# One inference step of a hybrid encoder: norm of the last tile, load of the convolution state and first sums of a down group rearranged

## The chip, the cores and the metric

The kernel runs on one core of a Trainium2 chip. The metric is the device time of one execution in microseconds. The engines are named as in the profile: PE (TensorE, matrix products), PEld (its weight loads), DVE (VectorE), ACT (ScalarE), POOL (GpSimd) and SP (SyncE, which issues most transfers). Lines such as L787 are lines of the kernel before.

## What is computed

One trunk layer over 1024 prompt frames and 32 sample frames (1056 columns in all, D_MODEL = 1024), all in float32:

```python
h = rmsnorm(x, g_mix) * (1 + sc1) + sh1
u = h @ w_in                                    # q, k, v, mLSTM parts, gates
ya = band_attention(...)                        # 8 heads of 64
xpad = concat([conv_left, qk_in])               # conv_left: state_conv for the sample, zeros for the prompt
conv = silu(sum(xpad[:, j:j + T] * conv_w[j] for j in range(4)) + conv_b)
...                                             # mLSTM, merge, output projection
x = x + gt1 * (merged @ w_out)
h2 = rmsnorm(x, g_ffn) * (1 + sc2) + sh2
g, up = split(h2 @ w_gate_up)
x = x + gt2 * ((silu(g) * up) @ w_down)         # d_ff = 2816, 22 rows of 128
y = x * rsqrt(mean(x * x) + 1e-6) * g_final     # the final norm
```

## The kernel before

**Tiling.** Activations lie with features on the 128 partitions and the 1056 frames on the free axis, cut in three thirds of 352 columns (`TILES`, `thirds`); `cut` = 704 is the start of the last third. Each float32 product is made of three passes over operands that are split in a high and a low part: `split_to` copies the high part on ACT (L394) and subtracts on DVE or POOL for the low part (L395).

**Order.** The order on PE, ACT, DVE and POOL is the order in which the program writes its instructions. SP's transfers are placed by the framework, as early as it reckons them to be free to start. `Weights` keeps a list of weight blocks: `use` calls `advance`, which loads and splits the blocks ahead, four tiles at most. Side jobs (attention, adaLN) are generators that are moved on by `side.tick()` between matmuls.

**Input projection.** `segs` is a list of segments; each calls a function first, then runs weight blocks while a side job goes on. Segment 3 (k, v, q of the last head pair and four gate blocks) comes before segment 4, which begins with `mlstm_setup` (L775): it fills `tri`, `maskbig` and other small tiles on POOL, loads the convolution state (24 rows of 128) into a scratch tile (L785), transposes it on PE (L787) and copies it to `scol` on DVE (L788). Then `vm_block(0)` starts its matmuls (L825).

**Down projection.** The first two thirds use 6 plain rows (`w_d0`, L1967) and two groups of 8 rows, each as 2x2 blocks with seven products instead of eight (`Seven`, `seven_down`). A product is 12 matmuls (`times`, L1726). Four of the seven products start on one of three fresh accumulators or go onto one in use: T2 and T3 onto B11's, B22 onto T1's, and T4 onto B11's again, after the second block of the next output; each finished product is added to the output rows by DVE (L1989). The operands of a group are sums of the activations (`subtract`, L1860, on DVE; for group 0 every other one on POOL) and are then split. The sums of the weight blocks are made by POOL (L1284).

**The plan.** This preparation is a list `steps` of (due beat, units, action), made by `plan_group`. `beside()` is called after each product of 12 matmuls and each fourth k step of the plain rows: it counts a beat (`through`) and runs the steps at the head of the list that are due, up to 2 units a beat (3 beside the plain rows). A fetch costs no unit, a sum or a split one. The list is strictly in order. Beat 12 (`BEFORE`) is the end of the last gate and up block, beat 36 (`FIRST`) the end of the plain rows. A group needs 8 fetches, 8 first sums, 4 splits (B11), 8 second sums and 24 splits; split results go to freed places, which have a due beat of their own (`free`).

**End.** The last third is done row by row, 8 rows (`w_d1`, L2082): 66 matmuls in three weight blocks (`chunks`), then x2 = acc * gt2 + x2 on DVE (L2090). Beside rows 0 to 6, `finish_some` norms the first two thirds. For the last third, `Finish` (three tiles of 128, 128 and 96 frames) transposes x2 back to frames (L2028), sums squares on ACT (L2029), sums, scales by 1/D, adds EPS and raises to -1/2 on POOL (L2036 to L2038), multiplies by the result and by g_final on DVE (L2044), and stores on SP (L2048). Rows 0 to 6 are taken before the last row's matmuls, row 7 after them.

## Time and profile before

| | us |
|---|---|
| median of three runs | 1645.67 |
| lowest and highest run | 1642.75, 1647.21 |
| the profiled execution | 1642.54 |
| its span, first to last instruction | 1640.6 |
| mean granted clock of PE | 0.995 |

The profile shows one execution. Its first part gives each engine's busy time; the waits say who stood for whom and for how long; the timeline lists instructions in order of time, merged where they repeat, with the idle time before them and what ended it in brackets; windows give the busy time of each engine in a stretch. A wait for several semaphores is put down to the one that came last.

### The profile page before, as it was taken

How to read it: one execution, taken by the hardware profiler on the slowest of the kernel's cores; microseconds unless marked ns; L12 is line 12 of the kernel's file. 1: busy time of each engine (PE TensorE's matmuls, PEld its weight loads, DVE VectorE, ACT ScalarE, POOL GpSimd, SP SyncE). 2: the span in 40 equal slices, each digit the busy share in tenths (PEclk: the TensorE clock that was granted, in tenths of full speed). 3: DMA queues.
4: the chain of work that ended last, by engine and by line, in shares of the span. 5: the costliest groups of instructions: out<-in, count | busy, mean ns of one | idle time of the engine just before them, and what ended most of it. 6: DMA issues, size and time to landing. Idle time of an engine off the chain costs nothing.

```text
span 1640.6 us, 27517 instructions
## 1 busy us (share of the span) xinstructions
PE 1589.7 (97%) x10324; PEld 1566.7 (95%) x10324; DVE 1121.0 (68%) x2100; ACT 780.8 (48%) x1732; POOL 535.7 (33%) x540
## 2 busy tenths in 40 slices
PE   7989999999999999999999998999999999999997
PEld 6989999999999999999999988999999999999997
DVE  6756564546776744546655689889888986698754
ACT  3456454543455544444434645454545444444443
POOL 1234333333332311000012155566565742233101
PEclk9999999999999999999999999999999999999999
DMA  9732323232222332584453211313222236427453
GB/s 344 251 98 75 111 75 106 67 126 75 84 83 78 67 94 66 131 273 152 128 151 109 91 53 39 105 53 104 79 82 88 78 102 216 141 65 238 134 157 123
DMA packets 210326, 192.45 MB, mean 117 GB/s; under 512 B 10570, under 2 KB 180530, under 8 KB 209170
## 3 DMA queue, kind: packets, MB, share of 16 engines
q1 hardware_dynamic: 205970, 188.60, 36.8%
q10 hardware_dynamic: 4224, 2.10, 0.4%
q8 instruction: 81, 1.33, 0.4%
q14 instruction: 51, 0.42, 0.1%
HBM read 152.19 MB, written 41.63 MB: 118 GB/s over the span
## 4 chain that ended last, share of the span: by engine, by line
PE 79%; DVE 8%; ACT 3%; issue 2%; DMA 1%; POOL 1%; DVEq 0%; POOLq 0%; ACTq 0%
PE mm L428 35%; PE psb L1726 24%; PE psb L2082 5%; PE mm L825 3%; PE psb L1967 3%; PE psV L725 2%; PE psS L667 1%; DVE wsp L395 1%; PE psT L694 1%; DVE s L395 1%; DVE s L1576 1%; DVE s L1989 1%; DVE sl L1563 1%; DVE st L681 1%; PE psV L1059 1%
## 5 line engine op out<-in xcount | busy, mean ns | idle before, releaser
L428 PE MATMUL mm<-s,wsp 128*128 128x352 f32 x4104 | 690.4, 324 | 5.8 <-DVE t L1657 1.9
L428 PEld LDWEIGHTS mm<-s,wsp 128*128 128x128 f32 x4104 | 656.8, 188 | 9.0 <-DVE stg L518 2.3
L1726 PE MATMUL psb<-s,wsp 128*128 128x352 f32 x2544 | 422.0, 323 | 11.4 <-DVE s L1989 5.5
L1726 PEld LDWEIGHTS psb<-s,wsp 128*128 128x128 f32 x2544 | 410.9, 189 | 14.4 <-issue 6.1
L395 DVE TENSOR_TENSOR wsp<-wraw,wsp 128x512 fp32r<-128x512 f32 (+1 forms) x284 | 246.0, 884 | 136.0 <-ACT wsp L394 134.2
L394 ACT ACTIVATE wsp<-wraw 128x512 fp32r<-128x512 f32 x340 | 201.5, 617 | 147.6 <-PE psb L1726 84.5
L687 POOL TENSOR_SCALAR st<-st,mx 128x640 f32<-128x640 f32 (+5 forms) x72 | 57.0, 791 | 193.7 <-DVE mx L686 179.5
L1141 DVE SCALAR_TENSOR_TENSOR t<-wa,cmix,t 128x512 f32<-128x512 f32 x112 | 88.8, 797 | 8.9 <-DMA wa<-in_w_ada_dram 8.5
L395 POOL TENSOR_TENSOR wsp<-wraw,wsp 128x512 fp32r<-128x512 f32 x56 | 73.8, 1339 | 52.4 <-ACT wsp L394 52.0
L2082 PE MATMUL psb<-s,wsp 128*128 128x352 f32 x528 | 86.7, 324 | 0.0
L2082 PEld LDWEIGHTS psb<-s,wsp 128*128 128x128 f32 x528 | 84.7, 188 | 0.0
L681 DVE CUSTOM_DVE_ANT_0 st<-psS,bias 128x640 f32<-128x640 f32 (+5 forms) x72 | 44.5, 618 | 57.8 <-PE psS L667 44.9
L1726 PE MATMUL psb<-x,wsp 128*128 128x352 f32 x432 | 80.2, 325 | 2.3 <-DVE x L1576 2.3
L682 ACT ACTIVATE st<-st,mx 128x640 f32<-128x640 f32 (+5 forms) x72 | 47.9, 666 | 67.5 <-DVE mx L681 67.5
L1676 POOL TENSOR_TENSOR t<-t,sl 128x352 f32<-128x352 f32 x18 | 17.4, 969 | 185.3 <-ACT sl L1674 185.3
L1726 PEld LDWEIGHTS psb<-x,wsp 128*128 128x128 f32 x432 | 71.5, 189 | 2.8 <-DVE x L1576 2.8
L701 ACT ACTIVATE pT<-psT 128x640 fp32r<-128x640 f32 (+3 forms) x80 | 38.7, 494 | 72.1 <-PE psT L694 55.1
L1764 DVE TENSOR_TENSOR t<-t,psb 128x352 f32<-128x352 f32 x120 | 60.4, 512 | 5.2 <-PE psb L1726 4.8
L1361 POOL TENSOR_TENSOR wraw<-wraw 128x512 f32<-128x512 f32 x25 | 37.1, 1482 | 76.8 <-DVE wsp L395 75.8
L706 DVE TENSOR_TENSOR pT<-psT,pT 128x640 fp32r<-128x640 f32 (+3 forms) x80 | 44.0, 559 | 20.5 <-ACT pT L701 20.4
L1361 POOL TENSOR_TENSOR wraw<-wraw,raw 128x512 f32<-128x512 f32 x33 | 55.8, 1704 | 0.9
L825 PE MATMUL mm<-s,s 128*128 128x264 f32 (+3 forms) x432 | 54.9, 283 | 0.0
(340 smaller groups left out, 2334.2 us busy)
## 6 DMA issues: line engine op xcount, KB each, us to landing
wraw<-in_w_in_dram SPq DMA_DIRECT2D x40, 512.0 KB
wraw<-in_w_gate_up_dram SPq DMA_DIRECT2D x33, 512.0 KB
wa<-in_w_ada_dram SPq DMA_DIRECT2D x64, 256.0 KB
wraw<-in_w_down_dram SPq DMA_DIRECT2D x32, 512.0 KB
a_d<-t SPq DMA_DIRECT2D x22, 528.0 KB
g_d<-t SPq DMA_DIRECT2D x16, 528.0 KB
x<-xres SPq DMA_DIRECT2D x16, 528.0 KB
t<-g_d SPq DMA_DIRECT2D x16, 528.0 KB
```

Source lines behind the costliest of these rows:

```text
L394: act.activation(dst[:, 0], src, AF.Copy)
L395: eng.tensor_tensor(dst[:, 1], src, f(dst[:, 0]), op=ALU.subtract)
L428: pe.matmul(pt[:, :hi - lo], wt[(w0 + k) // 4][:, a, (w0 + k) % 4], xt[k][:, b, lo:hi], start=(k == 0 and q == 0), stop=(k == n - 1 and q ...
L681: dve.tensor_tensor_reduce(so, sv, bi, -1.0, 3.0e38, ALU.add, ALU.min, mx[:n, 1:2])
L687: pool.tensor_scalar(st[:n, :w], st[:n, :w], mx[:n, 3:4], 1.0, op0=ALU.mult, op1=ALU.mult)
L825: pe.matmul(pt[:n, :wd], hs[k][:, a, i * P:i * P + n], whl[b][:, k, :wd], start=(k == 0 and q == 0), stop=(k == KD - 1 and q == 2))
L1141: dve.scalar_tensor_tensor(ac[:, c], wa, cmix[:, c, k:k + 1], ac[:, c], op0=ALU.mult, op1=ALU.add)
L1361: pool.tensor_tensor(a(dst), a(x), a(y), op=op)
L1726: pe.matmul(acc, wt[:, a, k], x[k][:, b], start=(start and not onto and k == 0 and q == 0), stop=(stop and k == 3 and q == 2), skip_group_ ...
L1764: dve.tensor_tensor(c, c, y, op=ALU.add if sign > 0 else ALU.subtract)
L1967: pe.matmul(acc, wt[k // 4][:, u, k % 4], piece_of[k, i][:, v], start=(k == 0 and q == 0), stop=(k == KP - 1 and q == 2))
L2082: pe.matmul(acc, wt[(k - k0) // 4][:, u, (k - k0) % 4], piece_of[k, 2][:, v], start=(k == 0 and q == 0), stop=(k == NF - 1 and q == 2))
```

## The change

The convolution state is loaded by a new function, `conv_state`, at the start of segment 3, into the first 24 rows of `tri`, and `mlstm_setup` begins with its transpose and copy, before `tri` is filled.

`plan_group` takes a beat for the first sums of its own (`sums_at`). Group 0 keeps its beats. Group 1's fetches are due at beat 27 and its 8 first sums at beat 30, where they were due at beats 36 and 38. Since the list is in order, the steps at the end of group 0 that are due at beat 36 or later (one split, which waits for a freed place) are put behind these sums (`behind`). All other steps of group 1 remain due at beat 38 or later.

For the last third a class `End` takes the place of the three `Finish`. Rows 0 to 6 are transposed and squared after the first weight block of the last row instead of before it (`ahead`). There POOL also adds their two partial sums and EPS (1/D is in the scale of the squares), and DVE multiplies the first 512 columns by g_final. After the last row (`last`), the last block is transposed and squared, POOL adds and takes the power tile by tile, ACT scales the first 512 columns and issues their stores on its own queue, DVE multiplies the other 512 by both factors, and SP stores them.

```diff
@@ -772,7 +772,13 @@
     qk = [None] * MH
     hm_n = [None, None]
 
+    def conv_state():
+        sp.dma_start(tri[:24], state_conv[0, 0].rearrange("j (r c) -> (j r) c", c=P))
+
     def mlstm_setup():
+        pt = mmt()
+        pe.transpose(pt[:, :24], tri[:24], ident[:24, :24])
+        dve.tensor_copy(scol, pt[:, :24])
         pool.memset(tri, 1.0)
         pool.affine_select(out=tri, in_=tri, compare_op=ALU.is_ge, fill=0.0, base=0,
                            pattern=[[1, P]], channel_multiplier=-1)
@@ -781,11 +787,6 @@
                            pattern=[[1, P]], channel_multiplier=-1)
         pool.memset(GT9, 0.0)
         sp.dma_start(bif, bass.AP(b_if.tensor, b_if.offset, [[0, P], [1, 8]]))
-        scr = tmpt((24, P))
-        sp.dma_start(scr, state_conv[0, 0].rearrange("j (r c) -> (j r) c", c=P))
-        pt = mmt()
-        pe.transpose(pt[:, :24], scr, ident[:24, :24])
-        dve.tensor_copy(scol, pt[:, :24])
         pool.memset(vms[:, :, :, P:P + 1], 1.0)
 
     def vm_block(pr):
@@ -1241,7 +1242,7 @@
         (nothing, b_qkv(0), None, 0),
         (nothing, mix(b_qkv(1), b_gates(0, 2)), lambda: attention(0), ATT_STEPS),
         (nothing, mix(b_qkv(2), b_gates(2, 4)), lambda: attention(1), ATT_STEPS),
-        (nothing, b_qkv(3) + b_gates(4, 8), lambda: attention(2), ATT_STEPS),
+        (conv_state, b_qkv(3) + b_gates(4, 8), lambda: attention(2), ATT_STEPS),
         (mlstm_setup, [vm_block(0), conv_block(0), conv_block(4), conv_block(1), conv_block(5)],
          lambda: attention(3), ATT_STEPS),
         (open_mls, [vm_block(1), conv_block(2), conv_block(6), conv_block(3), conv_block(7)],
@@ -1845,7 +1846,7 @@
         steps.append((max(need, after), 1, run))
         return x
 
-    def plan_group(g, fetch_at, work_at):
+    def plan_group(g, fetch_at, sums_at, work_at, behind=()):
 
 
         def block(p, i):
@@ -1855,16 +1856,17 @@
             src = a_d[KP + g * KD + p][:, :cut]
             steps.append((fetch_at, 0, lambda: sp.dma_start(x2[p][:, :cut], src)))
 
-        def subtract(dst, x, y):
+        def subtract(dst, x, y, at=work_at):
             eng = pool if g == 0 and len(steps) % 2 else dve
-            steps.append((work_at, 1, lambda: eng.tensor_tensor(block(*dst), block(*x), block(*y), op=ALU.subtract)))
+            steps.append((at, 1, lambda: eng.tensor_tensor(block(*dst), block(*x), block(*y), op=ALU.subtract)))
 
         for p in range(KD):
             fetch(p)
 
         for p in range(4):
-            subtract((p, 2), (p, 1), (p, 0))
-            subtract((p, 1), (p + 4, 1), (p, 1))
+            subtract((p, 2), (p, 1), (p, 0), sums_at)
+            subtract((p, 1), (p + 4, 1), (p, 1), sums_at)
+        steps.extend(behind)
         freed = [split_step(work_at, block(p, 0), operands[g]["B11"], p) for p in range(4)]
         for p in range(4):
             subtract((p, 0), (p + 4, 1), (p, 2))
@@ -1883,8 +1885,13 @@
         for k in range(KP):
             for i in range(2):
                 free.append((FIRST, split_step(4, x2[k][:, thirds[i]], piece_of, (k, i))))
-        plan_group(0, 9, BEFORE + 2)
-        plan_group(1, FIRST, FIRST + 2)
+        plan_group(0, 9, BEFORE + 2, BEFORE + 2)
+
+
+        behind = []
+        while steps[-1][0] >= FIRST:
+            behind.insert(0, steps.pop())
+        plan_group(1, FIRST - 9, FIRST - 6, FIRST + 2, behind)
         at = FIRST + 28
         raws = {}
 
@@ -2047,6 +2054,50 @@
                     out = y_sample[0, u - S:v - S] if q else y_prompt[0, u:v]
                     sp.dma_start(out[:, cs], y[u - self.a:v - self.a, cs])
 
+    class End:
+
+
+
+        def __init__(self):
+            self.cuts = [(a, min(a + P, T)) for a in range(cut, T, P)]
+            self.py = [(bank(512), bank(512)) for _ in self.cuts]
+            self.st = sl_pool[0].tile([P, 4, 3], F32, tag="est", name=nm("est"), bufs=1)
+            pool.memset(self.st, 1.0)
+            self.ys = [tmpt((P, D)) for _ in self.cuts]
+
+        def take(self, j0, j1, part):
+            for i, (a, b) in enumerate(self.cuts):
+                h, n = j0 // 4, b - a
+                py = self.py[i][h]
+                for j in range(j0, j1):
+                    pe.transpose(py[:n, (j - 4 * h) * P:(j - 4 * h + 1) * P], x2[j][:, a:b], ident)
+                act.activation(self.ys[i][:n, j0 * P:j1 * P], py[:n, (j0 - 4 * h) * P:(j1 - 4 * h) * P], AF.Square,
+                               scale=D ** -0.5, accum_out=self.st[:n, part, i:i + 1])
+
+        def ahead(self):
+            self.take(0, 4, 0)
+            self.take(4, KD - 1, 1)
+            st = self.st
+            pool.tensor_tensor(st[:, 0], st[:, 0], st[:, 1], op=ALU.add)
+            pool.tensor_scalar(st[:, 0], st[:, 0], 1.0, EPS, op0=ALU.mult, op1=ALU.add)
+            for y, py, (a, b) in zip(self.ys, self.py, self.cuts):
+                dve.tensor_tensor(y[:b - a, :512], py[0][:b - a], gB[:b - a, :512], op=ALU.mult)
+
+        def last(self):
+            self.take(KD - 1, KD, 2)
+            st = self.st
+            for i in range(3):
+                pool.tensor_tensor(st[:, 0, i:i + 1], st[:, 0, i:i + 1], st[:, 2, i:i + 1], op=ALU.add)
+                pool.tensor_tensor(st[:, 3, i:i + 1], st[:, 0, i:i + 1], mhalf[:, 0:1], op=ALU.pow)
+            for i, (y, py, (a, b)) in enumerate(zip(self.ys, self.py, self.cuts)):
+                n, r = b - a, st[:b - a, 3, i:i + 1]
+                act.activation(y[:n, :512], y[:n, :512], AF.Copy, scale=r)
+                dve.scalar_tensor_tensor(y[:n, 512:], py[1][:n], r, gB[:n, 512:], op0=ALU.mult, op1=ALU.mult)
+                for eng, cs in ((act, slice(0, 512)), (sp, slice(512, D))):
+                    for q, u, v in col_segments(a, b):
+                        out = y_sample[0, u - S:v - S] if q else y_prompt[0, u:v]
+                        eng.dma_start(out[:, cs], y[u - a:v - a, cs])
+
     def finish_some(ranges):
         for j in range(KD):
             dve.scalar_tensor_tensor(x2[j][:, :cut], cs[j], gt2[:, 0, j:j + 1], x2[j][:, :cut],
@@ -2069,9 +2120,7 @@
     for j in range(KD):
         if j == KD - 1:
             side.drain(job)
-            ends = [Finish(a, min(a + P, T)) for a in range(cut, T, P)]
-            for x in ends:
-                x.take(0, j)
+            end = End()
         acc = bank()
         for w, (k0, k1) in zip(w_d1[j], chunks):
             wt = W.use(w)
@@ -2084,16 +2133,14 @@
                 if k % 2 == 1:
                     side.tick()
             W.used(w)
+            if j == KD - 1 and k0 == 0:
+                end.ahead()
         while steps:
             steps.pop(0)[2]()
         for c, a, b in col_segments(cut, T):
             dve.scalar_tensor_tensor(x2[j][:, a:b], acc[:, a - cut:b - cut], gt2[:, c, j:j + 1], x2[j][:, a:b],
                                      op0=ALU.mult, op1=ALU.add)
-    for x in ends:
-        x.take(KD - 1, KD)
-        x.scale()
-    for x in ends:
-        x.put()
+    end.last()
     close_sl()
     pb_cm.__exit__(None, None, None)
```

## Rows read from the trace of the kernel before

**Rows 1.** The page, part 1: busy us, share of the span, instructions.

```profile
PE 1589.7 (97%) x10324; PEld 1566.7 (95%) x10324; DVE 1121.0 (68%) x2100; ACT 780.8 (48%) x1732; POOL 535.7 (33%) x540
```

**Rows 2.** Waits of PE, whole span: us in total, times, longest.

```profile
PE psb L1726 <- DVE s L1989: 5.5, 4, 2.7
...
PE mm L787 <- DMA t<-in_state_conv_dram: 2.2, 1, 2.2
```

**Rows 3.** Timeline at the conv state: start, us, engine, line, tiles, idle before.

```profile
371.13 0.21 POOL L776 MEMSET tri<- 128x128 f32 x1
...
372.62 0.32 SPq L785 DMA_DIRECT2D t<-in_state_conv_dram  x1
...
374.28 0.24 PE L787 MATMUL mm<-ident,t 24*128 24x24 f32 x1 [2.18 <-DMA t<-in_state_conv_dram]
```

**Rows 4.** Timeline of PE alone, first down group of seven products.

```profile
1429.98 15.73 PE L1726 MATMUL psb<-s,wsp 128*128 128x352 f32 x96 [2.73 <-DVE s L1989]
1446.02 8.28 PE L1726 MATMUL psb<-s,wsp 128*128 128x352 f32 x48 [0.30 <-DVE s L1989]
1455.54 23.51 PE L1726 MATMUL psb<-s,wsp 128*128 128x352 f32 x145 [1.24 <-DVE s L1989]
```

**Rows 5.** Timeline of DVE and POOL in the same stretch.

```profile
1414.81 1.39 DVE L395 TENSOR_TENSOR wsp<-wraw,wsp 128x512 fp32r<-128x512 f32 x2 [3.67 <-ACT wsp L394]
...
1420.01 1.30 POOL L1284 TENSOR_TENSOR t<-wraw,wraw 128x512 f32<-128x512 f32 x1 [4.96 <-issue]
...
1425.20 2.18 DVE L1860 TENSOR_TENSOR x<-x 128x352 f32<-128x352 f32 x2
...
1428.33 1.07 DVE L1860 TENSOR_TENSOR x<-x 128x352 f32<-128x352 f32 x2
1429.32 0.51 DVE L1989 TENSOR_TENSOR s<-s,psb 128x352 f32<-128x352 f32 x1
...
1431.35 0.51 DVE L1989 TENSOR_TENSOR s<-s,psb 128x352 f32<-128x352 f32 x1
...
1434.41 0.96 DVE L395 TENSOR_TENSOR s<-x,s 128x352 fp32r<-128x352 f32 x2
...
1442.29 3.15 DVE L1860 TENSOR_TENSOR x<-x 128x352 f32<-128x352 f32 x2
```

**Rows 6.** Timeline of SP's own queue, the second group's fetches and a load.

```profile
1404.74 1.48 SPq L1856 DMA_DIRECT2D x<-a_d  x3
1411.16 5.48 SPq L1268 DMA_DIRECT2D wraw<-in_w_down_dram  x2
```

**Rows 7.** Windows: length, busy of PE, PEld, DVE, ACT, POOL, clock, DMA share, GB/s.

```profile
1404.00:1416.00 12.00, 12.00 (x76) 12.00 (x75) 3.99 (x6) 3.73 (x8) 5.42 (x4) 1.00 0.71 236
```

**Rows 8.** Timeline of the last row and of the tail.

```profile
1617.19 0.60 ACT L2029 ACTIVATE t<-psb 128x512 f32<-128x512 f32 x1 [2.75 <-PE psb L2028]
1617.31 1.60 PEld L2028 LDWEIGHTS psb<-ident,x 128*128 128x128 f32 x15 [0.23 <-DVE x L2090]
...
1620.31 1.68 ACT L394 ACTIVATE wsp<-wraw 128x512 fp32r<-128x512 f32 x3
...
1631.27 0.20 POOL L2036 TENSOR_TENSOR fst<-fst 128x1 f32<-128x1 f32 x1 [12.65 <-ACT t L2029]
...
1631.83 0.55 POOL L2038 TENSOR_TENSOR fst<-fst,mhalf 128x1 f32<-128x1 f32 x1
...
1632.41 4.09 DVE L2044 SCALAR_TENSOR_TENSOR t<-psb,fst,t 128x512 f32<-128x512 f32 x6 [1.92 <-POOL fst L2038]
...
1633.19 4.97 SPq L2048 DMA_DIRECT2D out_dram<-t  x8
```

**Rows 9.** Windows of the tail, two halves of the stores.

```profile
1634.25:1636.75 2.50, 0.00 (x0) 0.00 (x0) 2.25 (x4) 0.00 (x0) 0.73 (x2) 0.50 1.01 382
1636.75:1639.25 2.50, 0.00 (x0) 0.00 (x0) 0.00 (x0) 0.00 (x0) 0.00 (x0) 0.50 0.66 164
```

**Rows 10.** Instructions of L525, issues on ACT's queue: ns min/median/max.

```profile
L525 ACTq DMA_DIRECT2D out_dram<-stg x8: 378/403/448, 77.6 to 298.5; - x8
```


## Prediction

> **What bounds the kernel now.** I read the busy times first: TensorE (PE) multiplies for 97% of the span [rows 1]. Time is therefore lost only where PE stands, so the second view is the list of PE's waits, and each part of the change is held against its line there [rows 2]. The third is the timeline around each wait, to see what PE stood for and what stood in front of that on the other engine: the conv state [rows 3], the first sums of the second down group [rows 4 to 7]. Last comes the timeline after PE's final matmul, where the chain runs DVE, POOL, DVE, SP, DMA and PE is idle anyway [rows 8 to 10].
>
> **Conv state.** The load of 12 KB is issued at 372.62, when PE has already finished the gate blocks, and PE's transpose starts at 374.28 after 2.18 us of idle time [rows 3]. After the change the load is issued one segment earlier, into `tri`, which nothing else uses yet; that segment is 7 weight blocks long, so it has landed. The transpose itself (0.24 us) stays. Removed: 2.2 us. Is something else late then? The first vm matmuls need `wl` from POOL, which was done before 371.13, since POOL had already begun its memsets then [rows 3]. POOL gets a new wait: memset of `tri` must follow PE's transpose (about 372.3), so POOL's memsets and selects begin 1.2 us later than 371.13, and so, at most, do the low halves of the next conv weights (L395) queued behind them; their matmuls come only after the whole vm block, nine units of work later. DVE's copy of the state, and what stood behind it, moves forward with PE. On SP one issue of 0.32 us goes from here to a place with nothing waiting on it. The scratch buffer that is no longer taken only frees a slot. I take **-2.2 us**; bounds -1.0 (those 1.2 us of POOL met in full) and -2.5 (the copy on DVE, 0.3, gained as well).
>
> **First sums of the second group.** Four waits of PE for DVE's adds make 5.5 us [rows 2]; three of them are 2.73, 0.30 and 1.24 us [rows 4], the fourth, the 1.2 us left of the 5.5, lies in the second group. I count in beats, one product of 12 matmuls: 23.51 us for 145 matmuls is 1.95 us a beat; the 96 matmuls from 1429.98 are beats 41 to 48, the 48 from 1446.02 beats 49 to 52 [rows 4]. With two units of planned work in it, DVE needs 2.03 us for a beat (from one add, 1429.32, to the next, 1431.35) [rows 5], more than PE, so its adds fall behind, and a product that goes onto an old accumulator must wait until the add has read it. Before: beats 38 to 51 carry two units each (8 first sums, 4 splits, 8 second sums, 7 splits: 27 units). After: 8 units are gone from there, 19 are left, in beats 38 to 47.
>
> The *later* waits, 0.30 (after beat 48) and 1.24 (after beat 52), fall when POOL's sums hold DVE up as well (two subtractions take 3.15 us at 1442.29) [rows 4, 5]. At that point the changed plan has nothing left for DVE but weights and adds, 1.1 us of a beat (2.03 less a pair of splits, 0.96 [rows 5]). I book both as gone: -1.5.
>
> The *first* wait, 2.73 us before beat 41, I do not book. Beat 41 adds B22's product onto T1's accumulator. The wait ends when DVE's add of 1429.32 is done (1429.83), and PE resumes at 1429.98 [rows 4, 5]. What stands before that add is beats 38 and 39, two units each. After the change they are still full: the four splits of B11 move up into them. A pair of splits takes 0.96 us where a pair of sums takes 1.07 [rows 5], so 0.2 us is won for two pairs, and the pair that took 2.18 took it because POOL was summing too [rows 5]. So about 2.5 us stays.
>
> *Where the 8 sums go:* beats 30 to 32, behind beat 28 or so of DVE's queue, from 1404.7 on. DVE is busy 3.99 of 12 us between 1404 and 1416 [rows 7], so 8.0 are free. 8 sums at 0.54 (half of 1.07 [rows 5]) are 4.3 us; POOL has four sums there [rows 7], and a pair on DVE that met POOL took 2.18 instead of 1.07 (1425.20 against 1428.33 [rows 5]), 1.1 more; four meetings make 8.7 us in the worst case, that is until 1416.7. Queued behind them on DVE are the low halves of the first group's first two weight blocks (1.39, at 1414.81 in the row [rows 5]), due at PE by 1419.4: done by 1418.1 at the worst. I take 0, and 1 us as the bound, for a last fetch that lands late. The sums wait for eight fetches. Their place in the plan moves from beat 36 to 27, but SP already issued the last of them at 1404.74 to 1406.2, long before beat 36 (1419) [rows 6]: SP's order is not the program's. The last should land by about 1413 (estimate: three of 128 x 704 words and the weight block issued just before them are 1.6 MB, 6.8 us at the 236 GB/s of this stretch [rows 7], from 1406.2). The load of 1411.16 and its successor wait for buffers that DVE's weight halves free, so they come up to 1.9 us later, and POOL's next sums with them (1420.01 [rows 5]), still within the two-unit beats. Sum for the group -1.5 - 0.2 = **-1.7 us**; bounds +1 (above) and -5.5 (all four waits go).
>
> **The last row.** The 21 transposes of the finished rows move from before the row's 66 matmuls to behind its first 24. PE does the same work; what goes is the wait for the previous row's DVE step, 0.23 us [rows 8]. The six squares on ACT took 3.1 us (1617.19 to 1620.31 [rows 8]) and now stand before the split of the row's third weight block. Before that block's turn PE has 24 matmuls, 3.9 us, and the transposes themselves, 1.6 us (the row of 1617.31); squares and the block's first split (0.6 on ACT, 0.7 on DVE) are 4.4. The three DVE multiplications (0.7 each, as in the tail) fit beside them. **-0.2**; bounds -0.3 and +0.6.
>
> **The tail.** Before: POOL's first add at 1631.27, power at 1631.83, then six DVE operations of 0.68 from 1632.41 to 1636.50, and SP's eight issues end at 1638.16 [rows 8]. The 1/D factor and EPS are now applied earlier, so the power follows 0.28 us sooner (DVE at 1632.1), and a tile costs POOL one add and one power, some 0.8 us: tiles are ready at 1632.1, 1632.9 and 1633.7. DVE does three operations instead of six and ends near 1634.5; SP issues four and ends near 1635.6. ACT scales the other halves (0.6 us each, as 128x512 copies [rows 8]) and issues in between, 0.40 us per issue of 128 rows [rows 10], the last two, of fewer rows, some 0.5: 1632.1 + 3 x 0.6 + 2 x 0.4 + 2 x 0.5 and waits of 0.3 give 1636.0. Issues thus end 2.1 us sooner. But the bytes also count. 352 rows of 4 KB are 1.44 MB. While the stores were of 128 rows the 16 DMA engines were full at 382 GB/s; in the second half, of 64 and 32 rows, they moved 164 GB/s at a busy share of 0.66, so full engines would move about 250 [rows 9]. 1.05 MB at 382 and 0.39 MB at 250 are 2.7 + 1.6 = 4.3 us; all at 382 are 3.8. The stores can begin near 1633.9 (0.3 sooner), so they end between 1637.7 and 1638.2, where they ended at 1639.25 [rows 9]: 1.0 to 1.6 sooner. I take **-1.3 us**; bounds -0.3 (a rival, below) and -2.1 (the issues alone).
>
> The Trainium skill's "DMA: Bandwidth & Descriptors" (section "Issuing engines are not separate DMA queues") speaks against this part: starting DMAs from several engines saves only the sequencer's issue time, usually small, since all run on the same 16 DMA engines. By that rule alone the second queue would bring almost nothing.
>
> **Sum.** -2.2 - 1.7 - 0.2 - 1.3 = -5.4 us. The profiled execution took 1642.54 for a span of 1640.6, so it would become 1637.1; it lies 3.1 us under the median of the runs, 1645.67, from which the prediction is made: **1640.3 us**, 0.33% faster. A measurement of this kernel can tell about 0.3%, 4.9 us, from no change.
>
> **Rivals.**
> *The first wait goes too* (13%). For it: two of the three operations ahead of the add were lengthened by POOL, and POOL's sums may come later. Against: the beats stay full. -5.4 - 2.5 gives 1637.8.
> *The second group wins nothing* (15%). POOL's sums, not DVE's, set the late waits: one pair took 3.15 us [rows 5]. -5.4 + 1.7 gives 1642.0.
> *The stores are bound by the DMA engines* (12%). In their second half they moved 164 GB/s, not 382 [rows 9]. If that rate belongs to transfers of 64 and 32 rows whoever issues them, the stores begin and end 0.3 us sooner: -5.4 + 1.0 gives 1641.3. Against: the engines were idle a third of that half, so SP's issues set the pace there. The page's rule named above would give this case.
> *Slower: the sums hold weights up* (10%). Place: DVE's queue between beat 28 and the first seven-product block. If SP puts five of the fetches behind the load it issued at 1411.16 [rows 6], which waits for a DVE half, the last lands not near 1413 but near 1421 (2.3 MB at 236 GB/s are 9.8 us), the sums end at 1422.5, and the first weight half behind them (0.7) makes PE wait 3.8 us from 1419.4; DVE begins the group with that lag, so the first wait can grow by 2.5 and the 1.5 of the late ones stays. Together +7.8, against -5.4: 1648.1. A landing up to 1416 costs nothing; from about 1419 on it outweighs the gains, and every us more adds one.
>
> **How the numbers follow.** Forecast 50% (38 of it past the bound, since 5.4 is only 0.5 us over it), the others as given; of the last, half lands later still and past the bound. Faster by over 0.3%: 38 + 13 = 0.51. Within: 12 + 15 + 12 + 5 = 0.44. Slower: 0.05. The range reaches from the first rival to the second and third and some way to the last, and takes in a median of three from runs that spread over 4.5 us (1.5 us each side): 1635.8 to 1644.4.
>
> **What would show it.** Right: no PE wait for the conv state; PE's wait near the fifth product of the first group still over 2 us, those at beats 48 and 52 gone; the eight subtractions of L1860 between 1404 and 1416; three DVE operations after the last POOL power and the stores ending 1.0 to 1.6 us sooner after PE's last matmul. Wrong: DVE's weight halves arriving after 1419 and PE waiting before the first product; ACT's split after the squares holding PE in the last row; new waits in the vm block; or SP's order of loads changed elsewhere, since it isn't the program's.

## The result, and the profile after

The changed kernel takes 1639.05 us (median of seven runs, six of them from 1636.95 to 1640.16), the kernel before, measured beside it, 1646.55 (seven runs from 1642.63 to 1652.42). The seventh run of the changed kernel took 5533.15 us and counts as disturbed: the ratio leaves it out. The ratio is 0.995, with a 95% interval of 0.9929 to 0.997. Forecast were 1640.3 us and 0.33% faster. The profiled execution took 1638.16 us for a span of 1636.4, where before had 1642.54 and 1640.6 [rows 1].

I cut each traced execution at six instructions that both kernels have, and give the length of each stretch in us. Each is a difference of two starts of PE instructions; the tail ends with the span.

| | before | after | difference | forecast |
|---|---|---|---|---|
| start to last gate matmul | 371.77 | 372.70 | +0.93 | 0 |
| to the last attention product (conv state) | 98.23 | 97.52 | -0.71 | -2.2 |
| to the first seven-product matmul | 949.39 | 949.44 | +0.05 | 0 |
| to the first matmul of the last third (groups) | 117.64 | 114.15 | -3.49 | -1.7 |
| to the last transposes (last third) | 93.36 | 93.21 | -0.15 | -0.2 |
| tail | 10.25 | 9.41 | -0.84 | -1.3 |

The first line I do not count as the change's: PE's waits for the input frames (L300) make 12.0 us after and 9.4 before, and this stretch is between 371.3 and 373.4 us in all thirteen kernels of this study. Without it the sum is -5.1 where -5.4 was forecast; but three of its terms are off, and two errors cancel.

**Conv state.** Timeline of after at the place of [rows 3] (start, us, engine, line, operation, tiles, idle time before and its releaser); the lines that make a chain:

```profile
372.95 0.24 PE L780 MATMUL mm<-ident,tri 24*128 24x24 f32 x1
...
373.25 0.21 POOL L782 MEMSET tri<- 128x128 f32 x1 [1.14 <-PE mm L780]
...
375.06 4.38 POOL L395 TENSOR_TENSOR wsp<-wraw,wsp 128x512 fp32r<-128x512 f32 x2
...
379.47 0.38 SPq L404 DMA_DIRECT2D wraw<-in_w_in_dram  x1
...
379.96 8.46 SPq L1137 DMA_DIRECT2D wa<-in_w_ada_dram  x3
...
385.03 0.75 DVE L1142 SCALAR_TENSOR_TENSOR t<-wa,cmix,t 128x512 f32<-128x512 f32 x1 [3.83 <-DMA wa<-in_w_ada_dram]
385.70 0.42 DVE L681 CUSTOM_DVE_ANT_0 st<-psS,bias 128x256 f32<-128x256 f32 x1
...
386.18 0.62 PE L667 MATMUL psS<-s,s 128*128 128x384 f32 x2 [1.29 <-DVE mx L681]
```

The transpose no longer waits: 2.18 us are gone. But 1.29 us (1.53 for the weight load) have come up at L667, 13 us later. Read backwards: PE waits for DVE's maximum (L681), which stands behind an adaLN product (L1142) that waits 3.83 us for its load; that load stands on SP's queue behind a load of weights (L404) that waits for a buffer POOL's halves free (L395); and those began later and took 4.38 us for two instead of 2.51. Since all of this execution runs 0.92 us late by then, I count from the start of the last gate matmul (372.70 here, 371.77 before): POOL's halves begin at 2.36 instead of 1.43, 0.93 us later, and the adaLN loads are issued at 7.26 instead of 4.51, 2.75 us later. Before, the same steps stood there:

```profile
373.20 2.51 POOL L395 TENSOR_TENSOR wsp<-wraw,wsp 128x512 fp32r<-128x512 f32 x2 [0.75 <-ACT wsp L394]
...
375.73 0.38 SPq L404 DMA_DIRECT2D wraw<-in_w_in_dram  x1
...
376.28 13.86 SPq L1136 DMA_DIRECT2D wa<-in_w_ada_dram  x4
```

**The groups.** Timeline of DVE in after, beside [rows 5]:

```profile
1406.80 1.52 DVE L1861 TENSOR_TENSOR x<-x 128x352 f32<-128x352 f32 x3 [1.87 <-DMA x<-a_d]
...
1410.22 6.78 DVE L1861 TENSOR_TENSOR x<-x 128x352 f32<-128x352 f32 x5
1416.92 1.28 DVE L395 TENSOR_TENSOR wsp<-wraw,wsp 128x512 fp32r<-128x512 f32 x2
...
1423.80 3.16 DVE L395 TENSOR_TENSOR s<-x,s 128x352 fp32r<-128x352 f32 x2
```

The first sums run at 1406.8 and 1410.2, and the weight halves behind them are done at 1418.2, where I had 1418.1 at the worst: five of the sums ran beside POOL's and took 6.78 us. In beat 38 now stand two splits of B11, 3.16 us for two beside POOL. Timeline of PE alone in after (its first two stops), then of PE's weight loads (PEld) in before and after, the lines whose idle time differs; two later gaps, of 0.2 and 1.0 us, stand in both:

```profile
1430.09 50.39 PE L1727 MATMUL psb<-s,wsp 128*128 128x352 f32 x312 [2.57 <-DVE s L1996]
1481.27 25.41 PE L1727 MATMUL psb<-s,wsp 128*128 128x352 f32 x157 [0.79 <-ACT wsp L394]
```

```profile
1429.95 15.47 PEld L1726 LDWEIGHTS psb<-s,wsp 128*128 128x128 f32 x96 [3.00 <-issue]
1445.98 3.99 PEld L1726 LDWEIGHTS psb<-s,wsp 128*128 128x128 f32 x25 [0.56 <-issue]
1450.33 3.67 PEld L1726 LDWEIGHTS psb<-s,wsp 128*128 128x128 f32 x23 [0.36 <-DVE wsp L395]
1455.51 23.25 PEld L1726 LDWEIGHTS psb<-s,wsp 128*128 128x128 f32 x145 [1.51 <-ACT wsp L394]
1479.57 3.67 PEld L1726 LDWEIGHTS psb<-s,wsp 128*128 128x128 f32 x23 [0.81 <-DVE wsp L395]
1484.74 25.16 PEld L1726 LDWEIGHTS psb<-s,wsp 128*128 128x128 f32 x157 [1.50 <-ACT wsp L394]
1510.93 1.74 PEld L1726 LDWEIGHTS psb<-s,wsp 128*128 128x128 f32 x11 [1.02 <-DVE wsp L395]
```

```profile
1430.06 50.14 PEld L1727 LDWEIGHTS psb<-s,wsp 128*128 128x128 f32 x312 [2.84 <-issue]
1481.24 25.15 PEld L1727 LDWEIGHTS psb<-s,wsp 128*128 128x128 f32 x157 [1.04 <-ACT wsp L394]
1507.70 1.75 PEld L1727 LDWEIGHTS psb<-s,wsp 128*128 128x128 f32 x11 [1.32 <-DVE wsp L395]
```

The first wait stays (2.57 where 2.73 stood in [rows 4]), and PE then runs 312 matmuls without a stop: the late waits are gone. The weight loads show more than the matmuls do: the gaps of these lines are 8.76 us before and 5.20 after. The 3.56 less are the late gaps (0.56 + 0.36 + 1.51 = 2.43), those of the second group near 1480 (0.81 + 1.50 against 1.04, so 1.27) and 0.16 of the first wait, less 0.30 that came up near 1507. The stretch became 3.49 shorter.

POOL's last weight sum ahead of the place near 1480, in before and in after:

```profile
1477.50 1.47 POOL L1284 TENSOR_TENSOR t<-wraw,t 128x512 f32<-128x512 f32 x1
```

```profile
1473.99 1.48 POOL L1285 TENSOR_TENSOR t<-wraw,t 128x512 f32<-128x512 f32 x1
```

It ends at 1478.97 before and at 1475.47 after.

**The tail.** Timeline of after, beside [rows 8], then windows of one us, the third to the sixth from the first store on, before and after (the last two columns are the busy share of the DMA engines and GB/s):

```profile
1628.75 0.72 ACT L2094 ACTIVATE t<-t,est 128x512 f32<-128x512 f32 x1 [0.49 <-POOL est L2091]
1628.75 2.31 DVE L2095 SCALAR_TENSOR_TENSOR t<-psb,est,t 128x512 f32<-128x512 f32 x3 [1.63 <-POOL est L2091]
...
1629.50 0.37 ACTq L2099 DMA_DIRECT2D out_dram<-t  x1
1629.53 3.08 SPq L2099 DMA_DIRECT2D out_dram<-t  x4
```

```profile
1635.19:1636.19 1.00, 0.00 (x0) 0.00 (x0) 1.00 (x2) 0.00 (x0) 0.00 (x0) 0.50 1.02 381
1636.19:1637.19 1.00, 0.00 (x0) 0.00 (x0) 0.31 (x1) 0.00 (x0) 0.00 (x0) 0.50 0.82 279
1637.19:1638.19 1.00, 0.00 (x0) 0.00 (x0) 0.00 (x0) 0.00 (x0) 0.00 (x0) 0.50 0.60 150
1638.19:1639.19 1.00, 0.00 (x0) 0.00 (x0) 0.00 (x0) 0.00 (x0) 0.00 (x0) 0.50 0.80 195
```

```profile
1631.50:1632.50 1.00, 0.00 (x0) 0.00 (x0) 0.00 (x0) 0.40 (x1) 0.00 (x0) 0.50 1.01 371
1632.50:1633.50 1.00, 0.00 (x0) 0.00 (x0) 0.00 (x0) 0.00 (x0) 0.00 (x0) 0.50 1.05 336
1633.50:1634.50 1.00, 0.00 (x0) 0.00 (x0) 0.00 (x0) 0.00 (x0) 0.00 (x0) 0.50 0.96 221
1634.50:1635.50 1.00, 0.00 (x0) 0.00 (x0) 0.00 (x0) 0.00 (x0) 0.00 (x0) 0.50 0.22 78
```

Counted from the last transposes (1630.40 before, 1627.01 after), the first store is issued at 2.79 before and 2.49 after, and the last one lands at 9.16 and 8.32. From the first issue to the last landing are 6.37 and 5.83 us. In the fourth to sixth us after the first issue the DMA engines were busy 0.82, 0.60 and 0.80 before; after, they are full for four us and then done.

### The profile page after: what moved, and what is told of

Read it like the earlier page. It is cut to its first block, busy times and chain, and to the rows that moved or that the text cites. A ratio compares the mean times of both kernels' runs of the same rounds, so it can differ in the third digit from the quotient of the medians.

```text
span 1636.4 us, 27518 instructions
## 1 busy us (share of the span) xinstructions
PE 1588.6 (97%) x10324; PEld 1567.1 (96%) x10324; DVE 1123.2 (69%) x2100; ACT 782.3 (48%) x1735; POOL 535.7 (33%) x537
## 4 chain that ended last, share of the span: by engine, by line
PE 82%; DVE 6%; ACT 3%; issue 2%; DMA 1%; POOL 0%; ACTq 0%; POOLq 0%; DVEq 0%
PE mm L428 36%; PE psb L1727 27%; PE psb L2131 5%; PE psb L1974 3%; PE mm L826 2%; PE psV L725 2%; PE psS L667 1%; PE psT L694 1%; DVE s L1577 1%; DVE wsp L395 1%; DVE sl L1564 1%; DVE st L681 1%; PE psV L1060 1%; ACT st L682 1%; PE psT L1062 1%
## 5 line engine op out<-in xcount | busy, mean ns | idle before, releaser
L395 DVE TENSOR_TENSOR wsp<-wraw,wsp 128x512 fp32r<-128x512 f32 (+1 forms) x284 | 245.4, 882 | 126.0 <-ACT wsp L394 124.1
L1142 DVE SCALAR_TENSOR_TENSOR t<-wa,cmix,t 128x512 f32<-128x512 f32 x112 | 89.2, 801 | 13.7 <-DMA wa<-in_w_ada_dram 13.4
L395 POOL TENSOR_TENSOR wsp<-wraw,wsp 128x512 fp32r<-128x512 f32 x56 | 75.6, 1371 | 51.3 <-ACT wsp L394 50.8
L681 DVE CUSTOM_DVE_ANT_0 st<-psS,bias 128x640 f32<-128x640 f32 (+5 forms) x72 | 44.4, 617 | 54.6 <-PE psS L667 42.2
L1362 POOL TENSOR_TENSOR wraw<-wraw 128x512 f32<-128x512 f32 x25 | 37.1, 1483 | 74.7 <-DVE wsp L395 73.8
```

The lines of the kernel that those rows point to most:

```text
L395: eng.tensor_tensor(dst[:, 1], src, f(dst[:, 0]), op=ALU.subtract)
L681: dve.tensor_tensor_reduce(so, sv, bi, -1.0, 3.0e38, ALU.add, ALU.min, mx[:n, 1:2])
L1142: dve.scalar_tensor_tensor(ac[:, c], wa, cmix[:, c, k:k + 1], ac[:, c], op0=ALU.mult, op1=ALU.add)
L1362: pool.tensor_tensor(a(dst), a(x), a(y), op=op)
```

## Experiments

All but the timed ones are single executions, which differ by 1 to 2 us in stretches that no edit touches. So I read the stretch that a kernel changes, not its total. Stretches with the same code differ less, but not by nothing: the changed conv part took 97.22 to 97.52 us (after, e4 to e7, e9), and the changed plan of the groups 113.77 to 115.26 where the granted clock stayed up (after, e2, e6, e7, e9). The stretches of all of them, in us:

| | to the last gate | conv | middle | groups | last third | tail | run |
|---|---|---|---|---|---|---|---|
| before | 371.77 | 98.23 | 949.39 | 117.64 | 93.36 | 10.25 | 1642.54 |
| after | 372.70 | 97.52 | 949.44 | 114.15 | 93.21 | 9.41 | 1638.16 |
| e1 conv part alone | 373.44 | 97.29 | 950.59 | 117.92 | 93.36 | 10.25 | 1644.88 |
| e2 state in another tile | 372.52 | 95.96 | 949.07 | 113.78 | 93.23 | 9.41 | 1635.72 |
| e3 group part alone | 372.29 | 98.68 | 950.90 | 115.14 | 93.36 | 10.23 | 1642.55 |
| e4 group 1 later | 372.25 | 97.50 | 950.60 | 113.41 | 93.21 | 9.39 | 1638.07 |
| e5 stores on one queue | 371.27 | 97.22 | 949.51 | 116.62 | 93.21 | 9.33 | 1638.86 |
| e6 short tile first | 371.97 | 97.35 | 949.81 | 114.05 | 93.34 | 9.76 | 1637.99 |
| e7 DVE scales alone | 371.64 | 97.50 | 949.38 | 113.77 | 93.22 | 9.16 | 1636.39 |
| e8 three repairs | 372.22 | 95.95 | 950.94 | 113.65 | 93.22 | 9.17 | 1636.89 |
| e9 whole rows | 371.76 | 97.37 | 950.75 | 115.26 | 93.22 | 9.29 | 1639.39 |
| e10 end part alone | 371.33 | 100.53 | 949.09 | 117.46 | 93.21 | 9.44 | 1643.00 |
| e11 longer conv wait | 371.48 | 105.28 | 950.97 | 118.96 | 93.36 | 10.21 | 1652.16 |

### The conv state: e1 and e2

e1 is the kernel before with the change's `conv_state` and `mlstm_setup`, and nothing else of it. e2 is the changed kernel with the tile replaced in load and transpose.

```diff
 e1 (on the kernel before)
+    def conv_state():
+        sp.dma_start(tri[:24], state_conv[0, 0]...)
-        (nothing, b_qkv(3) + b_gates(4, 8), ...
+        (conv_state, b_qkv(3) + b_gates(4, 8), ...
 e2 (on the changed kernel)
-        sp.dma_start(tri[:24], state_conv[0, 0]...)
+        sp.dma_start(gt[:24, 0], state_conv[0, 0]...)
```

> The kernel before with the load of the convolution state alone changed. Stage measured: from PE's last 24 gate matmuls to the matmuls after PE's wait near 443 us. Theory (the memset of tri now waits for PE, POOL's weight halves come later, SP holds the next weight load and the adaLN load behind it, DVE waits for that one): the 2.2 us wait is gone, a new wait of PE of 1.2 to 1.6 us stands before the third scores near 385, the stage is 0.7 us shorter, plus or minus 0.2. Rival (the new wait of the changed kernel comes from its other parts or from its later start): no new wait, the stage is 2.2 us shorter.

> The changed kernel with the state loaded into rows of gt, which POOL does not write, instead of tri. Theory: POOL's memsets need not wait for PE, its weight halves start within 0.5 us of their place in the kernel before, the adaLN load is issued some 2 us or more sooner than in the changed kernel, PE's wait near 385 falls to 0.3 us or less, and the stage is 2.2 us shorter than before (1.3 to 1.5 shorter than in the changed kernel). Rival (PE comes 2.2 us sooner to scores whose adaLN work on DVE has its own pace): the wait near 385 stays above 1 us and the stage is 0.5 to 1.0 us shorter than before.

e1 has the new wait too (1.06 us at L667 for DVE's maximum, a little under what I expected, with the adaLN product waiting 3.60 us for its load): its conv stretch is 0.94 us shorter than before's. So the conv part makes that wait by itself. In e2 POOL starts to fill `tri` when it did before, since nothing else lies in it. Timeline of e2:

```profile
371.89 0.21 POOL L782 MEMSET tri<- 128x128 f32 x1
...
378.48 10.69 SPq L1137 DMA_DIRECT2D wa<-in_w_ada_dram  x4
...
382.69 0.75 DVE L1142 SCALAR_TENSOR_TENSOR t<-wa,cmix,t 128x512 f32<-128x512 f32 x1 [1.55 <-DMA wa<-in_w_ada_dram]
...
384.46 0.60 PE L667 MATMUL psS<-s,s 128*128 128x384 f32 x2
```

The load comes 5.96 us after the last gate matmul (372.52 here) instead of 7.26, 1.3 us sooner where I expected 2, DVE waits 1.55 us instead of 3.83, and PE not at all. The stretch is 2.27 us shorter than before's: the whole wait is won. That settles it: it was the choice of `tri`, a tile that POOL had to fill, that gave back 1.5 of the 2.2 us. POOL's halves meet DVE and take 4.01 us in e2 too, and 1.45 us of SP's delay stay there without harm; the 1.1 us of POOL's own wait were what tipped it.

### The groups: e3 and e4

e3 is the kernel before with the change's plan of the groups and nothing else. e4 is the changed kernel with all of group 1 but its fetches and first sums three beats later.

```diff
 e3 (on the kernel before)
-        plan_group(1, FIRST, FIRST + 2)
+        plan_group(1, FIRST - 9, FIRST - 6, FIRST + 2, behind)
 e4 (on the changed kernel)
-        plan_group(1, FIRST - 9, FIRST - 6, FIRST + 2, behind)
+        plan_group(1, FIRST - 9, FIRST - 6, FIRST + 5, behind)
```

> The kernel before with the plan of the second group alone changed. Stage measured: from the first seven-product matmul (1419.4 before) to the first matmul of the last third. Theory: the whole 3.5 us that this stage lost in the changed kernel come from this part, the first wait of 2.6 us stays, the waits near 1446 and 1455 go: 3.3 to 3.7 us shorter. Rival (the two waits near 1480, which the prediction did not count on, went because PE came at another time relative to the weight loads): only 1.7 to 2.3 us shorter, with waits of over 1.5 us near 1480.

> The changed kernel with the rest of group 1's plan due at beat 41 instead of 38. Theory (the first wait stays because B11's four splits move into the beats 38 and 39 that the first sums leave): with nothing but weights and adds on DVE in beats 37 to 40 the wait of 2.6 us near 1427 falls under 0.5 us; the two-unit beats now end with beat 50 and meet POOL's sums near 1442 to 1449, so 0.5 to 1.5 us of waits come back there; net 1 to 2 us shorter than the changed kernel. Rival (the first wait is POOL's and the weight halves' doing): it stays above 2 us, net 0.

In e3 the weight-load gaps are like those of the changed kernel (2.87 first, nothing until 1483, then 0.81 and 1.09): the plan alone takes the late waits away and keeps the first. Its stretch is 2.5 us shorter, not 3.5, because the granted clock was lower behind the first wait (0.73 from 1430 to 1435; see the last experiment). In e4 the timeline of PE alone begins:

```profile
1420.34 31.04 PE L1727 MATMUL psb<-s,wsp 128*128 128x352 f32 x192
1452.20 23.51 PE L1727 MATMUL psb<-s,wsp 128*128 128x352 f32 x145 [0.82 <-DVE s L1996]
1476.33 3.98 PE L1727 MATMUL psb<-s,wsp 128*128 128x352 f32 x23 [0.62 <-DVE wsp L395]
1481.53 25.41 PE L1727 MATMUL psb<-s,wsp 128*128 128x352 f32 x157 [1.23 <-DVE s L1996]
```

With the splits of B11 out of beats 38 and 39 the first wait is gone altogether, which confirms why it stayed. Little of its 2.6 us is kept: PE, which comes sooner now, waits 0.82, 0.62 and 1.23 us further on, at places where the kernel before stood. The stretch is 113.41, 0.74 us under that of after but only 0.36 under the shortest of the same plan (113.77 in e7); 1 to 2 us were expected, and how much of the 0.74 is the edit's one execution does not tell.

### The tail: e5, e6, e7, e9 and e10

All but e10 are the changed kernel with an edit in `End.last`; e10 is the kernel before with the class `End` and nothing else.

```diff
 e5
-                for eng, cs in ((act, slice(0, 512)), (sp, slice(512, D))):
+                for eng, cs in ((sp, slice(0, 512)), (sp, slice(512, D))):
 e6 (in take and in last)
-            for i in range(3):
+            for i in (2, 0, 1):
 e7 and e9
-                act.activation(y[:n, :512], y[:n, :512], AF.Copy, scale=r)
+                dve.tensor_scalar(y[:n, :512], y[:n, :512], r, None, op0=ALU.mult)
 e10 (on the kernel before, with End.ahead behind the first weight block)
-            ends = [Finish(a, min(a + P, T)) for a in range(cut, T, P)]
+            end = End()
 e9 besides
-                        eng.dma_start(out[:, cs], y[u - a:v - a, cs])
+                    (act, sp)[i % 2].dma_start(out, y[u - a:v - a])
```

> The changed kernel with all eight last stores issued by SP; ACT and DVE still scale one half each. Measured: from PE's last transpose matmuls (the three after the last row) to the end of the stores and of the span. Theory (the issues set the pace): SP's eight issues take 4.5 to 5 us from the first tile on, as before, so the stores end 0.9 to 1.3 us later than in the changed kernel, and only the earlier start and DVE's shorter chain is left of the gain. Rival (the 16 DMA engines set the pace, whoever issues): 0.3 us later or less.

> The changed kernel with the tile of 96 frames taken first in the tail instead of last. Its stores go in pieces of 64 and 32 rows, whose issues take 0.5 and 0.6 to 1.0 us each instead of 0.35. Theory (what is left of the tail hangs on the last, slow issues): the last issue ends 0.7 to 0.9 us sooner, but ACT and SP come later to the full tiles by as much; the stores end 0 to 0.4 us sooner. Rival (the bytes set the end): no change within 0.1 us.

> The changed kernel with the first halves scaled by DVE too; ACT only issues. Theory (two engines that scale matter): DVE does six operations, three of 0.72 and three of 0.3 to 0.6 us, its chain of the tail grows from 2.3 to 3.2 to 3.9 us, and the stores end 0.6 to 1.2 us later than in the changed kernel. Rival (the issues or the bytes hide it): 0.3 us or less.

> The changed kernel, with both halves scaled on DVE and each segment of frames stored by one transfer of 4 KB rows, tiles in turn on the queues of ACT and SP: four transfers of the same 1.44 MB where there were eight of 2 KB rows. If the stream of 5.8 us from the first issue to the last landing is set by the bytes, it stays within 0.3 us of that while the first issue comes about 0.7 us later (a tile is stored only when both its halves are done): the tail takes about 9.7 us. If it is set by the count of rows or of transfers, the stream falls towards 5 us or less and the tail to 9.0 or less.

> The kernel before with the part of the last tile's norm alone. If the gain of the tail belongs to this part and to nothing else, the last third takes 93.2 us and the tail 9.4 (93.36 and 10.25 in the kernel before), and the stages ahead of them are those of the kernel before: 98.2 between gate and attention, 117.6 for the seven products, within 0.3 us where the granted clock is the same. If the tail's gain hung on the load on the DMA engines that the other parts move, it would differ from 9.4 by more than 0.2.

e5 takes 9.33 us with all eight stores on SP, no more than with two queues (9.41). SP's eight issues take 4.28 us there, some 0.5 apart, and the DMA engines are still full from the second us on. Windows of e5:

```profile
1631.34:1632.34 1.00, 0.00 (x0) 0.00 (x0) 0.53 (x1) 0.51 (x1) 0.00 (x0) 1.00 1.00 381
1632.34:1633.34 1.00, 0.00 (x0) 0.00 (x0) 0.00 (x0) 0.00 (x0) 0.00 (x0) 0.62 1.03 383
1633.34:1634.34 1.00, 0.00 (x0) 0.00 (x0) 0.00 (x0) 0.00 (x0) 0.00 (x0) 0.50 1.04 315
```

So the second queue brought nothing here, and my reason for the gain falls. What starved the DMA engines before was in the first place not SP but DVE: six operations of 0.68 us, which released the stores one after the other. SP issued each of the first five within 0.03 us of the end of one of them, and only the last three at its own pace; in e5 all eight go out at that pace, in 4.28 us instead of 4.97. Now ACT and DVE scale side by side. Two things remain open: ACT pays for its issues with its scaling (its third half is ready 4.89 us after the transposes in after, 4.02 in e5), so e5 measures the second queue's net, and with DVE's old chain a second queue was not run. The time from the first issue to the last landing is 5.72 us in e5, 5.83 in e7 and after, 5.54 in e9 with four transfers of whole rows: within 0.3 us the same, whoever issues and in how many pieces. That fits the 1.44 MB as the cause, but no run moved fewer bytes. Whatever starts the first store sooner then ends the tail sooner. e7 shows that, against my expectation of 0.6 to 1.2 us more: DVE's scaling of a half takes 0.49 us where ACT's takes 0.72, the first store is issued 2.25 us after the transposes instead of 2.49, and the tail is 0.25 shorter. In e9 the first store comes at 2.91 and the tail is 0.13 longer than in e7, 0.3 being won back in the stream and 0.2 behind the last landing; it is neither of the two outcomes that I expected. e6 (short tile first) is 0.35 longer, where I expected 0 to 0.4 less: the large stores are then last, and one issued at 1632.34 still has 2.84 us to go (the stream is 6.19 us).

e10 shows that the end part by itself is worth what it is in the whole: 93.21 and 9.44.

### The three repairs together: e8

e8 is the changed kernel with the edits of e2, e4 and e7.

> The changed kernel with the three repairs that the earlier runs showed: the state in a tile that POOL doesn't write (1.5 us between the last gate matmul and the last attention product), group 1 due three beats later (0.7 us in the stage of the seven products), both halves of the last scaling on DVE (0.25 us in the tail). If these are separate mechanisms they add up: 2.5 us under the changed kernel, so about 1636.5 where that had 1639.05, a ratio of 0.993 to 0.995 to the kernel before. If the waits that were moved in the group come back when the stages before it end sooner, the stage of the seven products is back at 114.1 and the sum is 1.8.

The median is 1636.91 us of five runs (1636.60 to 1637.83), a ratio of 0.9946 to the kernel before, with an interval of 0.9932 to 0.9959. The three stretches are 95.95, 113.65 and 9.17, together 2.3 us under the changed kernel's. Conv and tail come out as in the single runs; the 0.5 us of the groups is not clear of what the same plan varies by (113.77 to 115.26), so that e4's edit wins anything is not shown. Against the 1639.05 of the changed kernel the median is 2.1 us lower, but the two intervals overlap, so that this version beats the changed kernel rests on the stretches of the conv state and the tail (1.8 us), not on the totals.

### The granted clock behind a stop: e11

In e10 the conv stretch is 100.53 us, 2.3 longer than before's, although nothing was edited there: PE stood 2.94 us for the state (before 2.18), and the 48 matmuls behind it took 7.64 us, where they take 6.1 in all the others but e11. e11 lengthens that stop in the kernel before:

```diff
+        scr2 = tmpt((24, P))
+        sp.dma_start(scr2, scr)
-        pe.transpose(pt[:, :24], scr, ident[:24, :24])
+        pe.transpose(pt[:, :24], scr2, ident[:24, :24])
```

> The kernel before with a longer wait for the convolution state: behind its load the 24 rows are copied once more by a transfer, from one scratch tile to another, and the transpose takes the copy. PE should stand some 2 us longer than the 2.2 to 2.9 us seen so far. Theory: a stop of PE of this length can lower its granted clock just behind it, as behind the 2.94 us in the run with the end alone, where the 48 matmuls that followed took 7.64 us where they take 6.1. Then with 4.2 us or more the clock behind the wait falls for certain, those 48 matmuls take 7.5 us or more, and the stretch from gate to attention is longer by 3.5 us or more than the 98.2 of the kernel before. Rival: the clock fell there for another reason. Then the 48 matmuls take 6.1 us, and the stretch is longer by 2 us, which is the added wait alone.

Timeline of PE in e11, and windows (the third column from the right is the granted clock):

```profile
379.36 0.30 PE L789 MATMUL mm<-ident,t 24*128 24x24 f32 x1 [7.55 <-DMA t<-t]
379.58 7.73 PE L827 MATMUL mm<-s,s 128*128 128x264 f32 x48
```

```profile
380.00:385.00 5.00, 5.00 (x31) 5.00 (x31) 3.63 (x5) 0.39 (x1) 0.00 (x0) 0.67 0.16 52
385.00:390.00 5.00, 5.00 (x44) 5.00 (x43) 2.20 (x8) 0.76 (x3) 0.92 (x1) 1.00 0.17 54
```

The second transfer cost more than the 2 us I expected: the stop is 7.55 us. SP issued it only at 376.21, behind a weight load of 375.42 that had waited for POOL. The granted clock falls within the stop and is still low behind it, and the 48 matmuls take 7.73 us, 1.6 more than at full clock. The stretch is 7.05 us longer, of which 5.4 are the wait and 1.6 the clock; the median of the runs, 1652.92, is 7.75 over the 1645.17 beside it. The same fall stands behind the first wait of the groups in e5, whose stretch is 2.5 us longer than after's with the same waits. Windows of e5, then of e8, which has no wait there:

```profile
1425.00:1430.00 5.00, 2.28 (x11) 2.01 (x10) 4.97 (x10) 0.63 (x1) 1.50 (x2) 0.78 0.00 0
1430.00:1435.00 5.00, 5.00 (x20) 5.00 (x19) 4.20 (x9) 0.63 (x1) 0.00 (x0) 0.54 0.36 105
```

```profile
1425.00:1430.00 5.00, 5.00 (x33) 5.00 (x32) 4.39 (x9) 3.06 (x7) 2.82 (x2) 1.00 0.08 20
1430.00:1435.00 5.00, 5.00 (x34) 5.00 (x33) 4.93 (x11) 1.91 (x5) 0.00 (x0) 1.00 0.29 85
```

0.54 is near the lower of the clock's two levels (1.2 GHz of 2.4): PE does 20 matmuls in 5 us there, and 34 at full clock.

## Why the prediction was right, and where its terms were not

The forecast, 0.33% faster at 1640.3 us, came out at 0.5% and 1639.05, inside the range of 1635.8 to 1644.4. Term by term:

- **Conv state, forecast -2.2, measured -0.7.** The step that failed is the reach of POOL's new wait. I followed the 1.2 us (measured: 1.14) to the low halves of the conv weights and stopped at their matmuls, nine units off. But the same halves free the buffer for which SP's next load waits, and behind that load, on the same queue, stand loads of another job. The bound of -1.0 did not hold either, as it priced the delay at its own length; on the way it grew to 2.75 us on SP (from 0.93 us on POOL's halves), because the halves now met DVE. PE's new stop, 1.29 us, stands among the matmuls of the vm block, one of the signs of being wrong that the prediction had listed.
- **First wait of the groups, forecast to stay at about 2.5.** It is 2.57; e4 shows that its cause is the one given, the splits that move up. That the size fits so well is partly luck: the first pair of splits, beside POOL, took 3.16 us and not 0.96, but DVE came to it 1.4 us sooner than to the sums before (1423.80 against 1425.20). The rival in which it goes too is out.
- **Late waits, forecast -1.5.** They are gone. But I read them from PE's matmuls (0.30 and 1.24); the gaps of the weight loads are 0.56, 0.36 and 1.51, and the stretch follows these: 2.4.
- **The fourth wait, left out.** I named the 1.2 us in the second group and gave it no term. Its gap and the one ahead of it fell from 2.31 to 1.04. The one ahead hangs on POOL's weight sums: in all six executions in which PE stops there (before, e1, e4, e8, e10, e11) it resumes 0.60 or 0.61 us after the last of them ends. In the changed kernel that end comes 3.5 us sooner (1475.47 against 1478.97) and PE only 2.3 sooner, so PE passes 1.15 us behind it, and in the six other executions without this stop 0.99 to 1.38 behind. Why the gap that remains is shorter than the fourth wait was stays open. Sum of the group: -3.5 instead of -1.7. The rival in which POOL's sums hold the late waits up is out for those (e3); for this place it named the right engine.
- **Sums holding weights up.** Nothing of it: from 1410.22 on the sums wait for no fetch, the halves behind them were done at 1418.2, and PE began the block at 1419.66. The reserve was 1.5 us. The sums themselves ended at 1417.0, past the 1416.7 of my worst case.
- **Last row, forecast -0.2, measured -0.15.** ACT's split after the squares started at 1620.93, and PE didn't wait for it.
- **Tail, forecast -1.3, measured -0.84.** Power and first store came 0.3 us sooner, as worked out. The failed step is the length of the stream: I took the middle between 4.3 us and 3.8 us (all bytes at 382 GB/s), against some 5.0 before. From its first to its last packet it ran 4.53 us, where it ran 5.14 before, so 0.6 us were won and not 1.0: even with the engines 0.96 busy the last pieces went at 221 GB/s. And the gain came mainly from DVE's operations, not from SP's issues. The Trainium skill's "DMA: Bandwidth & Descriptors" (section "Issuing engines are not separate DMA queues") says that a second issuing engine saves only issue time. e5 agrees: 9.33 us with one queue, 9.41 with two. The rival of stores bound by the DMA engines was thus right that a second issuer does not shorten the stream; its price (0.3 us won) took the second half of before's stores for full engines, and these were not full.

That the total was nearly right owes something to luck: +1.5 in the first term and +0.5 in the last stand against -1.8 in the group. The measured medians lie 7.5 us apart, the two traces only 4.4. A part of the rest may be the clock: the traced execution of before lost none behind its two long stops, and of nine runs of before those from 1643.5 to 1645.5 us had a mean granted clock of 0.994 to 0.996, those from 1646.4 on 0.990 to 0.993. Where the clock fell in those runs no trace shows.

## What to carry to other kernels

When a step is moved into a tile or a queue place of another engine, follow that engine's delay through the buffers it frees and the loads behind them, not only to its own results; a scratch tile that POOL did not write cost nothing here. Read PE's stops at the weight loads as well as at the matmuls, and give every stop you name a term in the sum. In a tail of stores look for what starves the DMA engines (here DVE's operations, one after the other) before adding queues, and then for what starts the first store.

## What the runs showed of the hardware

- A stop of PE costs more than its length in some executions. Of 14 stops of 2.2 to 2.94 us at the two places above, four (2.60 in e3, 2.72 in e5, 2.92 in e11, 2.94 in e10) had a lower granted clock behind them, 0.54 to 0.80 in the lowest window of 5 us; ten, up to 2.73 us, had not. Measured prices: 1.5 us in e10, some 2.5 in e5, 1.6 behind e11's 7.55 us. Where the stop was gone (nine kernels at the conv state, e4 and e8 at the groups) the clock stayed at 1.00. Whether this widens a kernel's spread the runs do not show: e8, with neither stop, lies within 1.2 us, the changed kernel within 3.2 and nine runs of before within 4.7, but four runs of e11, with both stops, lie within 1.2 too.
- POOL and DVE lengthen one another: two weight halves on POOL took 2.51 us before and 4.38 after, where they ran beside DVE's two operations of L645, which took 3.60 instead of 2.53; two splits on DVE took 3.16 us beside POOL's sums and 0.95 without. The Trainium skill's "SBUF — State Buffer" (section "Who interferes with whom") describes a port pair that the two share under an exclusive lock; these rows agree in that both engines lose time, and do not show the lock itself.
- 12 KB copied once more from one scratch tile to another kept PE waiting 5.4 us more (2.18 before, 7.55 in e11). The copy was issued 3.1 us after the load (376.21 against 373.10), behind a load of weights on the same queue, and PE started 3.15 us after that; how much of this is the copy's own time no run tells apart.
